# Gate rows by a DRAM round trip, shift and scale columns by sums with ones and a DRAM turn

## The chip, the cores and the metric

The kernel runs on one core of one Trainium2 chip. The metric is the device time of one execution in microseconds (us). The core has engines that run side by side, each in the order of its own list of instructions: TensorE (PE, matrix products, with its weight loads shown apart as PEld), VectorE (DVE), ScalarE (ACT), GpSimd (POOL) and SyncE (SP), which here does no arithmetic and issues nearly all DMAs. Tiles live in SBUF (128 partitions); products land in PSUM, which is read by DVE and ACT. DRAM is reached by DMA alone.

## The reference

The computation is a backbone of two layers over 1024 latent tokens and 256 context tokens, 1024 channels wide, in 32-bit floats. Layer 0 mixes tokens by windowed attention, layer 1 by gated linear attention; each is followed by a squared-ReLU MLP with 4096 hidden channels. What matters for the change is the modulation. Each layer has six vectors of 1024 numbers for each of two streams (latent and context tokens): shift, scale and gate for the mixer, and shift, scale and gate for the MLP.

```python
def modulate(x, gain, shift, scale):
    return rms_norm(x, gain) * (1 + scale) + shift

m_lat = jnp.split((c_lat @ w_mod[i] + b_mod[i])[:, None, :], N_MOD, axis=-1)   # c_lat = silu(c)
m_ctx = jnp.split(c_con @ w_mod[i] + b_mod[i], N_MOD, axis=-1)                 # c_con = silu(c_ctx)
h_lat = modulate(x_lat, g_pre_mix[i], m_lat[0], m_lat[1])
x_lat = x_lat + m_lat[2] * rms_norm(y_lat, g_post_mix[i])
f_lat = channel_mlp(modulate(x_lat, g_pre_mlp[i], m_lat[3], m_lat[4]), w_mlp_in[i], w_mlp_out[i])
x_lat = x_lat + m_lat[5] * rms_norm(f_lat, g_post_mlp[i])
```

Context tokens go through the same with `m_ctx` in layer 0; layer 1 needs of them only what its mixer reads. The output is the latent stream.

## The kernel before

**How the work is staged.** Tokens are handled in ten tiles of 128 (two of context, eight latent). The stages follow one another: the first modulation vectors and the query, key and value projections; attention over blocks of 128 queries; the output projection of attention; the first MLP, hidden part and then output part; layer 1's gates, projections, backward and forward scan; its output projection; the second MLP. Large products are made from operands that are split in a high and a low part (`split`, L211: ACT makes the high part, DVE the rest) and take three products each (`mm3`, L225: lines 228, 229 and 230). The MLPs use seven products of quarters in place of eight.

**The modulation vectors.** Only the first two (shift and scale of layer 0's mixer) are needed at once and are made by products with the weight (`mod_first`, L363); the change doesn't touch them. The other ten are made beside other work by `mod_sums` (L287): for vector j of layer l, eight slices of the weight, 128 rows by 1024 columns (512 KB), are loaded one after the other (L297), and DVE adds each, times the 128 numbers of the conditioning vector that belong to its rows, to an accumulator of 128 x 1024 for each stream (L308, L310). The vector itself is the sum of an accumulator over its 128 partitions. Vectors 0 to 2 of a layer belong to its mixer, 3 to 5 to its MLP, in the order shift, scale, gate. All vectors of layer 0 and vectors 0 and 1 of layer 1 have two streams, the others one. `mod_sums` is a generator: each `next` gives the place in the program of one step. Vectors 2, 3 and 4 of layer 0 are made during projections and attention, vector 5 and all six of layer 1 during the hidden part of the first MLP, with the last step in its output part.

**Shift and scale** (`mod_columns`, L320) are needed with channels on the partitions, as 8 columns of 128 for each stream. Eight blocks of an accumulator are transposed on PE against the identity into two PSUM banks (L331), DVE sums each bank along its free axis (L332), and then adds the bias (L336) and, for a scale, one and the gain (L339). They are read by `modulated` (L429), which normalises and transposes a tile and applies them.

**Gates** (`mod_gate`, L342) are needed as rows over channels, the same in all partitions. Four products with a 128 x 32 tile of ones (L355) put the two halves of each stream's sum into four groups of 32 partitions of one PSUM bank; a vector with one stream is put there twice. DVE adds the bias and multiplies by the post-norm gain (L359, L360), which have been loaded into the same places (L353, L354), and leaves the tile `gm`. When a gate is wanted, `gate_rows` (L406) spreads a row over 128 partitions: a product of one column of the identity, repeated 128 times, with `gm` copies one row of it into all rows of a PSUM bank (L414), and ACT copies that bank into the tile `row` (L415), twice for a row of 1024. It is called six times: for both streams at the end of attention (`o_ready`), for both in the first MLP's output part (`gla_first`), and for the latent stream in layer 1's last scan and in the second MLP's output part. The rows are read by DVE at L470 (`post_norm`), L1852, L2018 and L2027.

**What sets the order.** Outside two stretches the program's order is only a priority: a planner with a model of the engines' times works out, from data and buffers, which instruction each engine takes next, so that a later one can come ahead of an earlier one that isn't ready. Its places are fixed when the kernel is built. The first stretch (the first projections, up to about 65 us) is in written order on all engines, the second (the last projections) on PE alone. In the MLPs the priority itself comes from a list of due times (`Timeline`, L77): a step's operands are to be split 5.2 us before its products (L1085), its weights loaded 8 us before that. SP's list holds loads of weights and tiles, stores of hidden values, and the DMAs of the modulation alike. Buffers are shared: 45 slots of 128 x 1024 (`u`), six half tiles of 128 x 512 (`half`), and in PSUM four single banks (`ps1`) and two double ones (`ps2`). In the output parts of the MLPs `bank` takes half of a double one.

Of the kernel before, what the change touches and what calls it, by code (L numbers as in the profile page):

```python
# [11 lines left out]
F32 = mybir.dt.float32  # L12
F32R = mybir.dt.float32r
AF = mybir.ActivationFunctionType
ALU = mybir.AluOpType
# [3 lines left out]
P = 128  # L19
# [145 lines left out]
class Backbone:  # L165
# [121 lines left out]
    def mod_sums(self, vectors, apart=False):  # L287
# [29 lines left out]
                self.mod_gate(l, j // 3, acc) if j % 3 == 2 else self.mod_columns(l, j, acc)  # L317
        yield

    def mod_columns(self, l, j, acc):  # L320

        nc = self.nc
        which = j // 3
        out = self.const([P, 2, KT], f"{'SG'[j % 3]}{l}{which}")
        for s, a in enumerate(acc):
            col = out[:, s, :]
            for q in range(2):
                pt = self.bank("modT")
                for c in range(4):
                    kk = 4 * q + c  # L330
                    nc.tensor.transpose(pt[:, P * c : P * (c + 1)], a[:, P * kk : P * (kk + 1)], self.ident)  # L331
                nc.vector.tensor_reduce(  # L332
                    out=col[:, 4 * q : 4 * (q + 1)], in_=pt.rearrange("p (c k) -> p c k", c=4), op=ALU.add,
                    axis=mybir.AxisListType.X,
                )
            nc.vector.tensor_tensor(col, col, self.bcol[:, l, KT * j : KT * (j + 1)], op=ALU.add)  # L336
            if j % 3 == 1:
                c0 = 16 * which + 8 * l
                nc.vector.scalar_tensor_tensor(col, col, 1.0, self.cols[:, c0 : c0 + KT], ALU.add, ALU.mult)  # L339
        self.pre.setdefault((l, which), [None, None])[1 - j % 3] = out  # L340

    def mod_gate(self, l, which, acc):  # L342

        nc, t = self.nc, self.t
        bias, gain = self.half("brow"), self.half("gp")
        c0 = D * (3 * which + 2)
        key = ("g_post_mix", "g_post_mlp")[which]
        ps = self.bank("mod")
        for s in range(2):
            for h in range(2):  # L350
                r = 32 * (2 * s + h)
                cs = slice(512 * h, 512 * (h + 1))
                nc.sync.dma_start(bias[r : r + 32, :], t["b_mod"][l, c0 : c0 + D][cs].partition_broadcast(32))  # L353
                nc.sync.dma_start(gain[r : r + 32, :], t[key][l, cs].partition_broadcast(32))  # L354
                nc.tensor.matmul(  # L355
                    ps[r : r + 32, :], self.ones, acc[s % len(acc)][:, cs], start=True, stop=True, tile_position=(0, r)
                )
        gm = self.const([P, 512], f"gm{which}")
        nc.vector.tensor_tensor(gm, ps, bias, op=ALU.add)  # L359
        nc.vector.tensor_tensor(gm, gm, gain, op=ALU.mult)  # L360
        self.gm[l, which] = gm

    def mod_first(self):  # L363

# [40 lines left out]

    def gate_rows(self, l, which, s):  # L406

        nc = self.nc
        gm = self.gm[l, which]
        row = self.u(s="grow")  # L410
        for j in range(2):
            r = 32 * (2 * s + j)
            pb = self.bank("grow")
            nc.tensor.matmul(pb, self.ident[:, r : r + 1].to_broadcast([P, P]), gm, start=True, stop=True)  # L414
            nc.scalar.copy(row[:, 512 * j : 512 * (j + 1)], pb)  # L415
        return row


# [1676 lines left out]
```

## Time and profile before

| | |
|---|---|
| median of 3 runs | 2607.4 us (2607.23 to 2610.37) |
| profiled execution | 2610.2 us, its span from first to last instruction 2608.5 us |
| granted clock of PE | 0.994 |
| busy: PE, PEld, DVE, ACT, POOL | 97%, 81%, 66%, 48%, 17% of the span |
| DMA | 348.62 MB, mean 134 GB/s |
| products with the identity for gate rows (L414) | 24 records, median 592 ns |
| transposes of accumulators (L331) | 80 records, median 272 ns |
| products with ones (L355) | 32 records, median 605 ns |
| DVE sums of transposed accumulators (L332) | 20, median 0.67 to 0.69 us |
| ACT copies of gate rows (L415) | 12, median 588 ns |

A row of a group names the line, the engine, the operation, what is written and read, and how often; then come times in ns. In a row of the timeline the start and the length come first, in us. In a row of waits the engine that waited stands first and what released it behind the arrow, then the total in us, how often, and the longest. A product of 32-bit floats that are not split leaves two records. Matmuls overlap one another, so the sum of their lengths is more than the time that they take up.

### The profile page before, as it was taken

The numbers are of one execution on the slowest core, as the hardware profiler recorded it, in microseconds if no ns is written. First come the engines' busy times: TensorE is split into PE (matmuls) and PEld (weight loads), VectorE is DVE, ScalarE is ACT, GpSimd is POOL, SyncE is SP. The second block draws the span as 40 slices with busy tenths as digits, with TensorE's granted clock in tenths as the row PEclk, the third lists the DMA queues.
The fourth block names the chain that finished last, engine by engine and source line by source line (L and its number), as shares of the span: only waits on it lengthen the run. The fifth ranks groups of instructions, "written<-read, shape, count | busy, mean of one in ns | idle before, by whom it ended". The sixth has DMA issues, their size and how long they took to land.

```text
span 2608.5 us, 36262 instructions
## 1 busy us (share of the span) xinstructions
PE 2543.1 (97%) x13523; PEld 2116.2 (81%) x13523; DVE 1714.7 (66%) x2607; ACT 1258.2 (48%) x2356; POOL 430.8 (17%) x720
## 2 busy tenths in 40 slices
PE   7999999999999999999999999999998999999998
PEld 5778888888888888788878888888887888878886
DVE  4775888757767665758868625636658656566676
ACT  3345777744644444433325535334446545445333
POOL 0354666411000000000002212212310000000002
PEclk9999999999999999999999999999999999999999
DMA  9210011222455565837245331102321554567474
GB/s 312 89 65 33 26 56 54 82 81 85 145 158 158 183 209 167 292 113 266 89 147 193 129 91 51 32 18 97 97 97 49 180 160 134 177 246 235 161 226 161
DMA packets 229856, 348.62 MB, mean 134 GB/s; under 512 B 24600, under 2 KB 123184, under 8 KB 229680
## 3 DMA queue, kind: packets, MB, share of 16 engines
q1 hardware_dynamic: 227088, 336.87, 39.8%
q0 software_dynamic: 2592, 9.44, 0.9%
q8 instruction: 106, 1.74, 0.3%
q14 instruction: 70, 0.57, 0.1%
HBM read 270.75 MB, written 75.50 MB: 133 GB/s over the span
## 4 chain that ended last, share of the span: by engine, by line
PE 85%; DVE 5%; DMA 4%; ACT 2%; issue 2%; POOL 1%; SPq 1%; DVEq 0%; POOLq 0%; ACTq 0%
PE p L229 7%; PE p L228 7%; PE p L230 6%; PE pa L229 4%; PE pa L228 4%; PE pa L230 4%; PE o L802 3%; PE y L230 3%; PE y L228 3%; PE y L229 3%; PE rp L228 2%; PE rp L229 2%; PE rp L230 2%; PE pc L228 2%; PE pc L230 2%; PE pt L783 2%
## 5 line engine op out<-in xcount | busy, mean ns | idle before, releaser
L229 PE MATMUL p<-ol,oh 128*128 128x512 f32 x896 | 350.7, 391 | 0.1
L230 PE MATMUL p<-oh,ol 128*128 128x512 f32 x896 | 347.2, 391 | 0.0
L228 PE MATMUL p<-oh 128*128 128x512 f32 x896 | 329.6, 392 | 4.9 <-ACT oh L212 4.1
L241 POOL TENSOR_SCALAR rs<-ss 128x1 f32<-128x1 f32 (+1 forms) x78 | 26.5, 340 | 1641.9 <-ACT later L235 1458.9
L213 DVE TENSOR_TENSOR ol<-wh,oh 128x1024 fp32r<-128x1024 f32 x128 | 153.5, 1222 | 94.3 <-ACT oh L212 93.9
L228 PEld LDWEIGHTS p<-oh 128*128 128x128 f32 x896 | 168.6, 189 | 44.1 <-ACT oh L212 5.4
L229 PEld LDWEIGHTS p<-ol,oh 128*128 128x128 f32 x896 | 168.9, 189 | 36.5 <-DVE ol L213 1.0
L230 PEld LDWEIGHTS p<-oh,ol 128*128 128x128 f32 x896 | 168.9, 189 | 35.3 <-issue 0.2
L212 ACT CAST oh<-wh 128x1024 fp32r<-128x1024 f32 x128 | 131.4, 1050 | 132.0 <-DVE wh L1212 27.6
L310 DVE SCALAR_TENSOR_TENSOR ma<-wm,cT,ma 128x1024 f32<-128x1024 f32 x112 | 147.2, 1345 | 47.0 <-DMA wm<-in_w_mod 47.0
L212 ACT CAST oh<-k 128x1024 fp32r<-128x1024 f32 x96 | 98.0, 1053 | 127.3 <-DMA k<-in_w_mlp_out 60.2
L213 DVE TENSOR_TENSOR wi<-wi,wi 128x512 fp32r<-128x512 f32 x176 | 116.6, 688 | 47.3 <-ACT wi L212 45.5
L1042 ACT COPY s<-pa 128x512 f32<-128x512 f32 x96 | 56.0, 585 | 185.5 <-PE pa L230 185.4
L767 POOL TENSOR_SCALAR pr<-pr,den 128x640 f32<-128x640 f32 (+2 forms) x160 | 124.3, 790 | 29.4 <-DVE den L765 16.6
L213 DVE TENSOR_TENSOR ol<-k,oh 128x1024 fp32r<-128x1024 f32 x96 | 113.9, 1224 | 21.2 <-ACT oh L212 17.3
L212 ACT CAST wi<-wi 128x512 fp32r<-128x512 f32 x176 | 103.4, 615 | 34.7 <-DMA hd<-h 20.9
L755 ACT ACTIVATE pr<-pr,nm 128x640 f32<-128x640 f32 (+1 forms) x128 | 102.5, 802 | 28.2 <-DVE nm L750 26.3
L228 PE MATMUL y<-woh,oh 128*128 128x512 f32 x288 | 113.9, 396 | 0.0
L230 PE MATMUL y<-woh,ol 128*128 128x512 f32 x288 | 112.4, 391 | 0.9 <-DVE ol L213 0.9
L229 PE MATMUL y<-wol,oh 128*128 128x512 f32 x288 | 112.2, 390 | 0.0
L229 PE MATMUL rp<-wgl,ah 128*128 128x512 f32 x288 | 112.1, 390 | 0.0
L230 PE MATMUL rp<-wgh,al 128*128 128x512 f32 x288 | 111.9, 390 | 0.0
(391 smaller groups left out, 6745.3 us busy)
## 6 DMA issues: line engine op xcount, KB each, us to landing
wm<-in_w_mod SPq DMA_DIRECT2D x96, 512.0 KB, 4.4
hd<-h SPq DMA_DIRECT2D x80, 512.0 KB, 3.0
wh<-hd SPq DMA_DIRECT2D x144, 256.0 KB, 3.7
wh<-in_w_mlp_out SPq DMA_DIRECT2D x144, 256.0 KB, 4.2
wi<-in_w_mlp_in SPq DMA_DIRECT2D x64, 512.0 KB, 5.0
k<-hd SPq DMA_DIRECT2D x80, 256.0 KB, 5.4
k<-in_w_mlp_out SPq DMA_DIRECT2D x80, 256.0 KB, 5.4
x<-in_x SPq DMA_DIRECT2D x16, 512.0 KB, 4.3
```

What stands on the lines that cost most here:

```text
L212: self.nc.scalar.copy(hi, src)
L213: self.nc.vector.tensor_tensor(lo, src, hi.bitcast(F32), op=ALU.subtract)
L228: mm(out, a[0], b[0], start=start, stop=False, skip_group_check=onto)
L229: mm(out, a[0], b[1], start=False, stop=False, skip_group_check=onto)
L230: mm(out, a[1], b[0], start=False, stop=stop, skip_group_check=onto)
L241: nc.gpsimd.tensor_scalar(r, ss, inv_n, EPS, ALU.mult, ALU.add)
L310: nc.vector.scalar_tensor_tensor(acc[s], raw, c, acc[s], ALU.mult, ALU.add)
L755: nc.scalar.activation(pr, pr, AF.Exp, bias=nm[:, e : e + 1], scale=-1.0, accum_out=sums[:, e : e + 1])
L767: nc.gpsimd.tensor_scalar(pr, pr, den[:, e : e + 1], 0.0, ALU.mult, ALU.add)
L783: nc.tensor.transpose(pt[:, P * j : P * (j + 1)], probs[e][:, P * kt : P * (kt + 1)], self.ident)
L802: nc.tensor.matmul(po[64 * e : 64 * (e + 1), P * i4 : P * (i4 + 1)], self.kv[tile_i // 2][:, tile_i % 2, 256 + HD * g : 256 + HD * (g + 1) ...
L1042: nc.scalar.copy(s["s", j], s["pa"])
```

## The change

Shift and scale vectors are summed over the partitions by products with ones, as gates are (`mod_rows`). ACT copies the bank into a half tile, one row of each group of 32 is stored to a DRAM tile of 2 x 2 x 512 (`to_dram`, one DMA of 2 KB for each row), and one DMA for each stream loads it back with channels on the partitions. Bias, one and gain follow as before. The transposes and the sums on DVE are gone.

Gates are stored to DRAM the same way once bias and gain are in. `gate_rows` is one DMA that reads the 4 KB of a stream into all 128 partitions; the products with columns of the identity and the copies on ACT are gone. A gate with one stream now fills two groups of partitions and not four, and loads half the bias and gain rows. `gm` was a constant tile and is now one of the half tiles. All new DMAs are issued by SP.

```diff
+    def mod_rows(self, acc):
+
+        ps = self.bank("mod")
+        for s, a in enumerate(acc):
+            for h in range(2):
+                r = 32 * (2 * s + h)
+                self.nc.tensor.matmul(
+                    ps[r : r + 32, :], self.ones, a[:, 512 * h : 512 * (h + 1)], start=True, stop=True, tile_position=(0, r)
+                )
+        return ps
+
+    def to_dram(self, rows, n):
+
+        d = self.dp.tile([2, 2, 512], F32, name=self.nm("md"))
+        for r in range(2 * n):
+            self.nc.sync.dma_start(d[r // 2, r % 2 : r % 2 + 1, :], rows[32 * r : 32 * r + 1, :])
+        return d
+
     def mod_columns(self, l, j, acc):
 
         nc = self.nc
-        which = j // 3
+        which, n = j // 3, len(acc)
         out = self.const([P, 2, KT], f"{'SG'[j % 3]}{l}{which}")
-        for s, a in enumerate(acc):
+        rows = self.half("mrow")
+        nc.scalar.copy(rows[: 64 * n], self.mod_rows(acc)[: 64 * n])
+        d = self.to_dram(rows, n)
+        for s in range(n):
             col = out[:, s, :]
-            for q in range(2):
-                pt = self.bank("modT")
-                for c in range(4):
-                    kk = 4 * q + c
-                    nc.tensor.transpose(pt[:, P * c : P * (c + 1)], a[:, P * kk : P * (kk + 1)], self.ident)
-                nc.vector.tensor_reduce(
-                    out=col[:, 4 * q : 4 * (q + 1)], in_=pt.rearrange("p (c k) -> p c k", c=4), op=ALU.add,
-                    axis=mybir.AxisListType.X,
-                )
+            nc.sync.dma_start(col, d[s].rearrange("h (k p) -> p (h k)", p=P))
             nc.vector.tensor_tensor(col, col, self.bcol[:, l, KT * j : KT * (j + 1)], op=ALU.add)
...
     def mod_gate(self, l, which, acc):
 
         nc, t = self.nc, self.t
-        bias, gain = self.half("brow"), self.half("gp")
+        n = len(acc)
+        bias, gain, gm = self.half("brow"), self.half("gp"), self.half("gm")
         c0 = D * (3 * which + 2)
         key = ("g_post_mix", "g_post_mlp")[which]
-        ps = self.bank("mod")
-        for s in range(2):
+        for s in range(n):
             for h in range(2):
                 r = 32 * (2 * s + h)
                 cs = slice(512 * h, 512 * (h + 1))
                 nc.sync.dma_start(bias[r : r + 32, :], t["b_mod"][l, c0 : c0 + D][cs].partition_broadcast(32))
                 nc.sync.dma_start(gain[r : r + 32, :], t[key][l, cs].partition_broadcast(32))
-                nc.tensor.matmul(
-                    ps[r : r + 32, :], self.ones, acc[s % len(acc)][:, cs], start=True, stop=True, tile_position=(0, r)
-                )
-        gm = self.const([P, 512], f"gm{which}")
-        nc.vector.tensor_tensor(gm, ps, bias, op=ALU.add)
-        nc.vector.tensor_tensor(gm, gm, gain, op=ALU.mult)
-        self.gm[l, which] = gm
+        m = slice(0, 64 * n)
+        nc.vector.tensor_tensor(gm[m], self.mod_rows(acc)[m], bias[m], op=ALU.add)
+        nc.vector.tensor_tensor(gm[m], gm[m], gain[m], op=ALU.mult)
+        self.gm[l, which] = self.to_dram(gm, n)
...
     def gate_rows(self, l, which, s):
 
-        nc = self.nc
-        gm = self.gm[l, which]
         row = self.u(s="grow")
-        for j in range(2):
-            r = 32 * (2 * s + j)
-            pb = self.bank("grow")
-            nc.tensor.matmul(pb, self.ident[:, r : r + 1].to_broadcast([P, P]), gm, start=True, stop=True)
-            nc.scalar.copy(row[:, 512 * j : 512 * (j + 1)], pb)
+        self.nc.sync.dma_start(row, self.gm[l, which][s].rearrange("h c -> (h c)").partition_broadcast(P))
         return row
```

## The prediction

> **What bounds the kernel now.** I read the totals and the chain of waits first, then the busy times by stage, then the single instructions that the change touches, and last the waits of TensorE (PE), VectorE (DVE) and the DMA queue of SyncE (SP).
>
> ```profile
> span 2608.5 us, 36262 instructions
> ...
> PE 2543.1 (97%) x13523; PEld 2116.2 (81%) x13523; DVE 1714.7 (66%) x2607; ACT 1258.2 (48%) x2356; POOL 430.8 (17%) x720
> ...
> PE 85%; DVE 5%; DMA 4%; ACT 2%; issue 2%; POOL 1%; SPq 1%; DVEq 0%; POOLq 0%; ACTq 0%
> ...
> 0.00:65.00 65.00, 49.48 (x417) 37.18 (x418) 30.89 (x71) 24.47 (x40) 4.44 (x22) 0.97 1.01 313
> ...
> 355.00:505.00 150.00, 146.91 (x1395) 125.41 (x1392) 123.59 (x262) 114.32 (x292) 90.41 (x165) 1.00 0.21 58
> ...
> 600.00:1050.00 450.00, 443.84 (x2343) 378.38 (x2342) 305.59 (x414) 226.53 (x420) 7.51 (x17) 1.00 0.51 160
> ...
> 1050.00:1380.00 330.00, 325.22 (x1420) 264.60 (x1419) 235.67 (x280) 124.28 (x133) 0.00 (x0) 1.00 0.53 182
> ...
> 2560.00:2608.00 48.00, 38.80 (x170) 31.46 (x168) 32.18 (x39) 14.12 (x26) 9.32 (x16) 0.96 0.57 203
> ```
>
> The last five rows are stages: their length, then busy time of PE, weight loads, DVE, ACT and POOL. PE is idle for 2608.5 - 2543.1 = 65.4 us, and the first and last stage hold 15.5 and 9.2 of them, which the change doesn't touch. In the 2495 us between it is idle for 40.7 us, 1.6%. So what PE no longer has to do should come off the end nearly one for one, as long as nothing else becomes late; DVE, 82% busy in the attention stage (355 to 505) and 68% in the first MLP, is the next.
>
> **What is removed from PE.** Busy time can't be added up here, since matmuls overlap; I take the distance from start to start, set against the 0.23 us at which the split weight products follow one another.
>
> ```profile
> L414 PE MATMUL grow<-gm,ident x24: 591/592/696, 501.4 to 2278.8; 128*128 128x512 f32 x24
> 501.36 3.70 PE L414 MATMUL grow<-gm,ident 128*128 128x512 f32 x8
> 504.89 0.82 PE L783 MATMUL pt<-ident,pr 128*128 128x128 f32 x6
> L331 PE MATMUL modT<-ident,ma x80: 270/272/329, 365.8 to 990.1; 128*128 128x128 f32 x80
> 953.40 0.39 PE L230 MATMUL pa<-o4h,wi 128*128 128x512 f32 x1
> 953.63 1.03 PE L331 MATMUL modT<-ident,ma 128*128 128x128 f32 x8
> ...
> 954.73 0.39 PE L229 MATMUL pa<-o6l,wi 128*128 128x512 f32 x1
> ```
>
> The 12 products with a column of the identity are 24 records. Eight of them hold PE from 501.36 to 504.89, 3.53 us, or 0.43 to 0.44 each: 24 x 0.43 = **-10.3 us**. Eight transposes push the second product behind them from 953.40 + 2 x 0.23 = 953.86 to 954.73: 0.87 us, 0.109 each, so 80 x 0.109 = **-8.7 us**.
>
> **What is added to PE.** The sum over partitions with ones is an operation the gates already do.
>
> ```profile
> 1359.26 0.39 PE L230 MATMUL p<-oh,ol 128*128 128x512 f32 x1
> 1359.58 1.05 PE L355 MATMUL mod<-ma,ones 128*32 128x512 f32 x4
> 1360.56 0.50 PE L228 MATMUL p<-oh 128*128 128x512 f32 x1
> 1360.89 0.39 PE L229 MATMUL p<-ol,oh 128*128 128x512 f32 x1
> 911.41 1.07 PE L355 MATMUL mod<-ma,ones 128*32 128x512 f32 x8
> 912.40 0.50 PE L228 MATMUL pc<-o3h,wi 128*128 128x512 f32 x1
> 912.74 0.39 PE L229 MATMUL pc<-o3l,wi 128*128 128x512 f32 x1
> ```
>
> Two products (four records) and four products (eight records) both hold PE for 0.98 to 0.99 us: products into different groups of 32 output rows run side by side. With the slower product behind it a piece costs 1360.89 - (1359.26 + 2 x 0.23) = 1.17, say 1.2 us. Six vectors get one (shift and scale of the MLP of layer 0, and of both halves of layer 1). If the four products of a vector with two streams stay together this is 6 x 1.2 = 7.2 us; if all four such vectors fall apart into pairs, 4 x 2.4 + 2 x 1.2 = 12.0. The gate at 911 stayed together, the one at 1359 came apart. I take together for the four vectors in the MLP stage, where 911 lies, and pairs for the two in attention, without the slower neighbour: 4 x 1.2 + 2 x 2.0 = **+8.8 us**. The last gate (layer 1, one stream) now has two products where it came in two pieces: **-1.2 us**. The other gate of layer 1 drops from four to two in one piece: nothing. Sum on PE: -10.3 - 8.7 - 1.2 + 8.8 = **-11.4**.
>
> [...]
>
> **Waits that go.**
>
> ```profile
> PE px L228 <- ACT grow L415: 1.5, 1, 1.5
> PE pt L783 <- DVE S L332: 0.7, 1, 0.7
> L332 DVE TENSOR_REDUCE S<-modT x10: 671/684/686, 369.2 to 955.4; 128x4 f32<-128x512 f32 x10
> L415 ACT COPY grow<-grow x12: 572/588/604, 502.5 to 2500.9; 128x512 f32<-128x512 f32 x12
> ```
>
> Both name removed instructions: **-2.2 us**. DVE loses 20 reductions of 0.68 us (13.7 us), ACT loses 12 copies and gains 6 of the same size. I count these at nothing: they lie beside PE's 98% in their stages. At the rate at which PE feels DVE's waits in the first MLP (13%, below) they would be worth 1.8 us more.
>
> **The DMAs that come.** 20 row stores of 2 KB, 10 column loads (1024 single floats each), 12 gate-row stores, 6 broadcasts of 512 KB, minus 8 bias and gain loads: 40 more issues on SP, which also issues every weight load.
>
> ```profile
> hc<-hx SPq DMA_DIRECT2D x64, 64.0 KB, 1.8
> gd<-in_gla_w_gate_down SPq DMA_DIRECT2D x8, 64.0 KB, 3.8
> x<-in_x SPq DMA_DIRECT2D x16, 512.0 KB, 4.3
> L339 DVE SCALAR_TENSOR_TENSOR G<-G,cols x5: 166/167/206, 501.2 to 993.6; 128x8 f32<-128x8 f32 x5
> L470 DVE TENSOR_TENSOR xo<-y,grow x18: 1214/1224/1226, 525.2 to 1968.6; 128x1024 f32<-128x1024 f32 x18
> 540.33 0.90 ACT L457 ACTIVATE h<-xt,S,G 128x128 f32<-128x128 f32 x2 [4.71 <-PE xt L438]
> SPq L1073 <- ACT hx L1004: 82.9, 25, 10.6
> DVE ma L310 <- DMA wm<-in_w_mod: 46.5, 29, 3.3
> ```
>
> A broadcast costs about what loading x does, 4.3 us, and its first use lies 525.2 - 502.5 = 22.7 us after the copy it replaces: hidden, also if it takes five times that. A store to DRAM lands after 1.8 us (64 KB row); the nearest row for a column load is the gate-down weight, 1024 pieces of 64 bytes, 3.8 us; a single float may go faster or, unseen, far slower. So columns come some 1.8 + 3.8 plus 1.6 to 2 of issue, 7 to 8 us, after the ACT copy. The MLP's scale columns are finished from 501.2 on now, and their first reader, at 540.3, is 39 us later.
>
> What can hurt is the queue. SP waits for ACT's copy, then for the store's landing, and behind it stand the next slice of the modulation weight (L297), MLP weights (L979) and hidden stores. DVE's addition of the bias waits for the column, and behind it stand the accumulations (L310) and splits (L213) that PE needs. The planner places an instruction where it expects it to be ready, so only its error counts. SP already waits for ACT 82.9 us in 25 places of the first MLP (the row before last), and DVE for a slice 46.5 us in 29, at most 3.3 each; PE loses 450.0 - 443.8 = 6.2 us there, 13% of what DVE waits. Six vectors at 3.3 us each give 19.8 on DVE and, at 13%, **+2.6 us**; the bounds are nothing and the second rival's 24.
>
> **Sum:** -11.4 - 2.2 + 2.6 = -11.0. The profiled execution took 2610.2 us (1.7 around its span), so 2599.2 for it; the median shown is 2.8 lower, so **2596.4** for the median, -0.4%. By stage: attention -3.7, first MLP's hidden part -0.4 (transposes -5.2, sums +4.8), its output part -6.1, the two places of layer 1 -1.7 each, and the 2.6 in the first two.
>
> **The rivals.**
>
> *The new order eats the gain.* From 65 us on the planner works out every place anew, and a freed PE slot is worth something only if the next operands are there.
>
> ```profile
> PE p L228 <- ACT oh L212: 4.1, 2, 2.6
> PE pa L228 <- ACT wi L212: 3.6, 2, 1.8
> PE pa L228 <- ACT o6h L212: 3.0, 1, 3.0
> 1243.32 1.02 PE L414 MATMUL grow<-gm,ident 128*128 128x512 f32 x2
> ```
>
> Waits of PE are few and single, up to 3 us; three or four more such would take the 11 us: 2607, no change. For it: six of the products, as at 1243, were placed long before their use, as fillers where the planner saw a hole. Against it: on the chip PE had no hole there. Chance 0.13.
>
> *DVE held by the columns (slower).* If the additions are placed as though a column were there at once, DVE stands for the whole 8 us, six times. The cover is the planned lead of the MLP's splits, 5.2 us ahead of their products (L1085).
>
> ```profile
> L213 DVE TENSOR_TENSOR wi<-wi,wi 128x512 fp32r<-128x512 f32 x176 | 116.6, 688 | 47.3 <-ACT wi L212 45.5
> L212 ACT CAST wi<-wi 128x512 fp32r<-128x512 f32 x176 | 103.4, 615 | 34.7 <-DMA hd<-h 20.9
> ```
>
> A split takes 0.6 + 0.7 = 1.3 us of it, so 3.9 us are covered and PE loses 4: 6 x 4 = 24, against -13.6 without the other waits: 2607.4 - 13.6 + 24 = 2618. It decides from a hold of 3.9 + 13.6/6 = 6.2 us per vector. For it: DVE is in order. Against it: no wait of DVE for a slice is above 3.3 us. Chance 0.08.
>
> *The columns themselves are slow.* [...] Chance 0.04. [...]
>
> **Range and chances.** Forecast 0.75, rivals 0.13, 0.08 and 0.04. A measurement of this kernel tells about 0.2% (5.2 us) from no change, so faster means below 2602.2: 0.75; same 0.13; slower 0.12. Low end: all sums together (7.2, not 8.8: -1.6), no added wait (-2.6), 1.8 more from DVE, and an order that is luckier by some 4: 2586. High end: all in pairs (+3.2) and the better half of the first rival: 2608. The forecast's own range is 2586 to 2602.
>
> **What would show it.** Right: no transposes of the accumulators and no products with the identity for rows, 64 records of products with ones instead of 32, PE busy time lower and its idle time between 65 us and the last stage near 40; DVE waits for column loads of 20 us or less in all; broadcasts land in 4 to 5 us. Wrong: column loads landing after tens of us, DVE waits of over 5 us per vector for them, weight slices waited for longer than 46.5 us in the first MLP, or the first MLP's hidden part longer by more than 3 us.

## The result and the profile after

The changed kernel takes 2595.1 us (median of 5 runs, 2591.74 to 2597.13) against 2607.4 for the kernel before (5 runs beside them, 2605.4 to 2610.37): ratio 0.995, 95% interval 0.9939 to 0.9961. The forecast was 2596.4. Of the six executions of rows_only below, one took 2821.9 us against 2592.2 to 2598.2 for the others, and it is left out of that version's median and ratio.

The first listing has the totals of the changed kernel and the stretch of its span from 65 us to the last stage: length, then busy time of PE, weight loads, DVE, ACT and POOL.

```profile
span 2595.4 us, 36179 instructions
...
PE 2529.4 (97%) x13451; PEld 2105.8 (81%) x13451; DVE 1703.1 (66%) x2587; ACT 1255.6 (48%) x2350; POOL 435.2 (17%) x720
...
65.00:2545.00 2480.00, 2437.87 (x12851) 2034.08 (x12850) 1638.96 (x2477) 1215.64 (x2282) 420.24 (x682) 0.99 0.40 129
```

The span is 13.1 us shorter. PE is busy 13.7 us less, and its idle time is 66.0 us, as good as the 65.4 of before; in the stretch shown it is 2480.0 - 2437.9 = 42.1, against 40.7 before. So in total PE's work came off the end one for one. The stages will show that this total hides larger terms of both signs.

The next two listings are from the groups by tile: the bank `mod` with its copy `mrow`, and the DRAM tiles `md` with those who waited for them.

```profile
L326 PE MATMUL mod<-ma,ones x64: 592/605/617, 127.0 to 1346.0; 128*32 128x512 f32 x64
...
L344 ACT COPY mrow<-mod x6: 568/582/592, 367.6 to 979.9; 128x512 f32<-128x512 f32 x4, 64x512 f32<-64x512 f32 x2
```

```profile
L335 SPq DMA_DIRECT2D md<-mrow x20: 233/245/253, 368.3 to 980.8; - x20
...
L419 SPq DMA_DIRECT2D grow<-md x6: 319/351/529, 497.1 to 2485.6; - x6
...
  DVE G L349: 3.1, 4
  DVE S L349: 1.5, 2
```

There are 64 records of products with ones, the transposes of accumulators and the products with the identity for rows are gone, and DVE waited 4.6 us in six waits for columns in the whole run. How long a broadcast takes to land, for which the prediction had 4 to 5 us, the profile doesn't record.

One column path in the timeline of the changed kernel, with the products that it stands between:

```profile
803.55 0.28 PE L230 MATMUL px<-ah,wi 128*128 128x256 f32 x1
...
803.76 1.06 PE L326 MATMUL mod<-ma,ones 128*32 128x512 f32 x8
...
804.75 0.50 PE L228 MATMUL pc<-o3h,wi 128*128 128x512 f32 x1
...
804.91 0.59 ACT L344 COPY mrow<-mod 128x512 f32<-128x512 f32 x1 [0.97 <-PE mod L326]
805.09 0.39 PE L229 MATMUL pc<-o3l,wi 128*128 128x512 f32 x1
...
805.53 1.12 SPq L335 DMA_DIRECT2D md<-mrow  x4
...
807.00 0.39 SPq L348 DMA_DIRECT2D S<-md  x1
...
809.20 0.17 DVE L349 TENSOR_TENSOR S<-S,bcol 128x8 f32<-128x8 f32 x1 [0.68 <-DMA S<-md]
```

Four products with ones are eight records in one piece, and the next product starts 0.99 us after them. The stores go out at 805.53, the load (of one stream's 1024 single floats) at 807.00, and DVE, which waited for it, starts at 809.20: 3.7 us from the first store and 2.2 from the load's issue.

For the stages I took the start of the first product of each (the first into `y`, then into `pa`, into the MLP's `p`, and so on; the last stage ends with the start of PE's last product) in two profiles of each kernel, the second being the runs before_again and after_again below. Lengths in us:

```
                    before   again | after    again | change of mean | forecast
up to output proj.   506.9   505.8 | 499.9    497.2 |     -7.8       |  -3.7
output projection    123.6   123.6 | 125.9    125.6 |     +2.2       |   0
first MLP, hidden    416.3   415.0 | 410.7    409.1 |     -5.8       |  -0.4
first MLP, output    400.9   402.6 | 396.7    397.6 |     -4.6       |  -6.1
layer 1 mixer        420.4   420.3 | 420.5    420.5 |     +0.2       |  -1.7
its output proj.     101.1   101.1 | 102.7    102.7 |     +1.6       |   0
second MLP, hidden   319.3   317.4 | 315.6    315.5 |     -2.8       |  -1.7
second MLP, output   310.6   309.5 | 314.2    314.6 |     +4.4       |   0
```

The +2.6 us of added waits stood beside the first and the third row. Two profiles of one kernel differ by up to 2.7 us in the first stage and by up to 1.9 in the others, so a change of under 2 us is taken as real only where the two profiles agree. Part of that difference may be the clock: without the last 20 us, the granted clock of PE is 0.50 in seven stretches of the first profile of before and in eight of the first of after, each 3.41 us long but for one of 6.83 in either profile. In the stretch from 1855.51 of after weight products follow one another at 0.43 us, and at 0.23 behind it. Layer 1's output projection takes 102.5 to 102.8 us with such a stretch and 101.1 or 101.2 without, so I put one at some 1.3 to 1.7 us; the section on the hardware has the rows.

### The profile page after: what moved, and what is told of

It reads as the page before. It is cut to its first block, busy times and chain, and to the rows that moved or that the text cites. A ratio compares the mean times of both kernels' runs of the same rounds, so it can differ in the third digit from the quotient of the medians.

```text
span 2595.4 us, 36179 instructions
## 1 busy us (share of the span) xinstructions
PE 2529.4 (97%) x13451; PEld 2105.8 (81%) x13451; DVE 1703.1 (66%) x2587; ACT 1255.6 (48%) x2350; POOL 435.2 (17%) x720
## 5 line engine op out<-in xcount | busy, mean ns | idle before, releaser
L229 PE MATMUL p<-ol,oh 128*128 128x512 f32 x896 | 349.8, 390 | 0.2
L228 PE MATMUL p<-oh 128*128 128x512 f32 x896 | 329.3, 392 | 8.6 <-ACT oh L212 5.4
L228 PEld LDWEIGHTS p<-oh 128*128 128x128 f32 x896 | 168.3, 188 | 47.0 <-ACT oh L212 8.6
L212 ACT CAST oh<-wh 128x1024 fp32r<-128x1024 f32 x128 | 131.5, 1050 | 154.5 <-DVE wh L1216 34.9
L229 PEld LDWEIGHTS p<-ol,oh 128*128 128x128 f32 x896 | 168.6, 188 | 36.4 <-DVE ol L213 1.5
L228 PE MATMUL y<-woh,oh 128*128 128x512 f32 x288 | 115.0, 400 | 2.5 <-ACT woh L212 1.3
L759 ACT ACTIVATE pr<-pr,nm 128x640 f32<-128x640 f32 (+1 forms) x128 | 102.5, 802 | 28.3 <-DVE nm L754 26.9
L229 PE MATMUL y<-wol,oh 128*128 128x512 f32 x288 | 112.6, 392 | 0.1
L229 PE MATMUL rp<-wgl,ah 128*128 128x512 f32 x288 | 112.0, 390 | 0.0
```

Of the source, the lines that this page charges most:

```text
L212: self.nc.scalar.copy(hi, src)
L228: mm(out, a[0], b[0], start=start, stop=False, skip_group_check=onto)
L229: mm(out, a[0], b[1], start=False, stop=False, skip_group_check=onto)
L759: nc.scalar.activation(pr, pr, AF.Exp, bias=nm[:, e : e + 1], scale=-1.0, accum_out=sums[:, e : e + 1])
```

## The experiments

All times are medians beside runs of the kernel before on the same chip (2606.4, 2607.9 and 2607.8 in the three groups).

| run | us | ratio to before, 95% |
|---|---|---|
| rows_only | 2595.6 | 0.9957 (0.9945 to 0.9970) |
| cols_only | 2600.6 | 0.9973 (0.9963 to 0.9983) |
| reductions_kept | 2598.8 | 0.9972 (0.9963 to 0.9980) |
| second_hop | 2595.2 | 0.9957 (0.9945 to 0.9969) |
| after_again | 2593.7 | 0.9951 (0.9937 to 0.9964) |
| rows_late | 2592.1 | 0.9943 (0.9930 to 0.9955) |
| rows_late_again | 2593.0 | 0.9942 (0.9928 to 0.9956) |
| pe_turn | 2595.5 | 0.9947 (0.9935 to 0.9960) |
| late_pe_turn | 2595.7 | 0.9954 (0.9941 to 0.9966) |
| one_store | 2595.6 | 0.9955 (0.9942 to 0.9967) |
| before_again | 2606.6 | one execution |

**rows_only: the gates alone.** The columns are made as before.

```diff
-        rows = self.half("mrow")                      # changed mod_columns
-        nc.scalar.copy(rows[: 64 * n], self.mod_rows(acc)[: 64 * n])
-        d = self.to_dram(rows, n)
...
+        nc.tensor.transpose(pt[:, P * c : P * (c + 1)], a[:, P * kk : P * (kk + 1)], self.ident)
+        nc.vector.tensor_reduce(out=col[:, 4 * q : 4 * (q + 1)], in_=pt.rearrange("p (c k) -> p c k", c=4), ...)
```

> The gate half of the change alone: gates go through DRAM and are spread by one DMA; shift and scale columns are made as before, with 80 transposes and 20 DVE reductions. Theory (PE's own time is what counts): products with the identity -10.1 us measured from start to start, last gate in one piece -1.2, wait for the copy of a gate row -1.5: -12.8, some 2594.6 us, ratio 0.995. Rival (much of the gain came from the columns, by DVE's relief or by the planner's new order, since the first MLP's hidden part alone got 5.7 us shorter): -6 to -8, some 2600, ratio 0.997 to 0.998. PE idle time stays near 65 us by the theory.

Measured: 2595.6, 10.8 us below the kernel before beside it (2606.4). The interval of the ratio is 7.8 to 14.3 us and holds the 12.8 of PE's account. The first MLP's hidden part keeps its length (414.1 against 416.3 and 415.0), its output part is 392.5, the shortest of all.

**cols_only: the columns alone.** `mod_gate` and `gate_rows` are those of before; the excerpt shows the second of them against the changed kernel.

```diff
-        self.nc.sync.dma_start(row, self.gm[l, which][s].rearrange("h c -> (h c)").partition_broadcast(P))
+        for j in range(2):
+            r = 32 * (2 * s + j)
+            pb = self.bank("grow")
+            nc.tensor.matmul(pb, self.ident[:, r : r + 1].to_broadcast([P, P]), gm, start=True, stop=True)
+            nc.scalar.copy(row[:, 512 * j : 512 * (j + 1)], pb)
```

> The column half alone: shift and scale by sums with ones and a DRAM turn; gates stay in a constant tile and are spread by 12 products with the identity and 12 ACT copies as before. Theory (PE's own time): transposes -8.7, six sums +7.0, wait for a reduction -0.7: -2.4, some 2605 us, ratio 0.999, not to be told from no change. Rival (DVE's relief or order): the hidden part of the first MLP is shorter by 5 to 6 us as in the whole change, and the time by 5 to 6: 2602, ratio 0.998.

Measured: 2600.6, 0.9973 (4.4 to 9.6 us faster). The 2.4 that PE's account gave lie outside that; the rival's 5 to 6 lie inside. Much of the gain is in the hidden part: 409.8 us against 415 to 416. The profiled execution, at 2596.7 us the fastest of its seven, has the stage up to the output projection 5 us shorter as well (501.3), so this one profile shows more than the median gains. And the halves don't add up: by the ratios 11.2 and 7.0 are 18.2 us, where both together gave 13.0 and 12.8 (after, after_again). The intervals all but allow that, but two places show that something is given back only with both. The output projection takes 123.1 us with the gates alone, 123.6 with the columns alone, 125.9 and 125.6 with both; rows_late below goes into it. The first MLP's output part takes 392.5 with the gates alone and 400.1 with the columns alone against a mean of 401.8 before, so 9.3 and 1.7 less, but 396.7 and 397.6 with both, 4.6 less; why is open.

The waits of PE from 600 to 1050 us, first in the kernel before, then in its second profile, then in the changed kernel, show where a good part of the hidden part's gain came from:

```profile
PE pc L228 <- DVE s L1046: 2.0, 1, 2.0
PE pa L228 <- ACT wi L212: 1.8, 1, 1.8
PE pc L228 <- ACT wi L212: 0.7, 1, 0.7
PE pc L230 <- DVE wi L213: 0.6, 1, 0.6
```

```profile
PE pc L228 <- DVE s L1046: 2.0, 2, 1.8
...
PE pc L228 <- ACT wi L212: 0.8, 1, 0.8
PE pc L230 <- DVE wi L213: 0.8, 1, 0.8
```

```profile
PE pa L228 <- ACT wi L212: 1.8, 1, 1.8
PE pa L229 <- DVE o6l L213: 0.5, 1, 0.5
PE px L228 <- ACT hx L1038: 0.5, 1, 0.5
```

Three kinds of wait, 3.3 us in one profile of before and 3.6 in the other, are not there in the changed kernel; the other 2 us or so of the gain they don't explain. The largest follows a slice of the modulation weight that landed late: DVE stood in its accumulation, the sum `s` was behind it on DVE, and PE needed `s`.

**reductions_kept: is it that DVE has less to do?** The 20 reductions of before run again, on the bank `mod`, with their result unused.

```diff
+        ps = self.mod_rows(acc)
+        idle = self.small(4, "idle")
+        for _ in range(2 * n):
+            nc.vector.tensor_reduce(out=idle[: 64 * n], in_=ps[: 64 * n].rearrange("p (c k) -> p c k", c=4),
+                                    op=ALU.add, axis=mybir.AxisListType.X)
```

> The changed kernel with DVE's 20 reductions of a 128 x 512 PSUM bank put back (13.7 us of DVE work whose result nobody reads, so the output is the same). Theory (DVE's work lies beside PE): 2595 us, within 2 us of the changed kernel, first MLP's hidden part within 1 us of 410.7. Rival (DVE's relief took the 3.4 us of idle PE time from the hidden part): hidden part about 414 us, time 2597 to 2599, and DVE's waits or PE's waits for DVE and ACT grow by that.

Measured: 2598.8, ratio 0.9972, some 4 to 5 us above the changed kernel; but not in the way that either account had it. The hidden part is 409.7, as short as without the reductions. In the profiled execution, the slowest of the ten at 2603.4 us, the clearest loss lies at the output projection: it takes 129.1 us (125.9 and 125.6 without). The waits of ACT and PE for its weights, and the stretch behind them with its granted clock:

```profile
ACT woh L212 <- DMA wor<-in_attn_w_o: 13.0, 3, 11.7
...
PE y L228 <- ACT woh L212: 3.2, 1, 3.2
```

```profile
511.50:518.50 7.00, 5.42 (x26) 4.09 (x26) 4.65 (x5) 5.05 (x6) 0.00 (x0) 0.53 0.52 161
```

PE waits 3.2 us for the first weights, where the changed kernel waits 1.3 (below), and over the 7.0 us shown the granted clock is 0.53, where the same stretch of the changed kernel has 1.00. So in this execution a longer wait at one place, and the lower clock behind it, are the largest part of the loss; how much of that stands behind the median isn't shown, nor why the wait is longer. That DVE's relief shortens the hidden part is out.

**second_hop: what the column path costs.** One more DMA, from DRAM to DRAM, lengthens every column's way.

```diff
-        d = self.to_dram(rows, n)
+        first = self.to_dram(rows, n)
+        d = self.dp.tile([2, 2, 512], F32, name=self.nm("md2"))
+        nc.sync.dma_start(d[:n], first[:n])
```

> The changed kernel with one more DMA between the store and the load of the columns (DRAM to DRAM, 4 or 8 KB), so that a column comes some 2 us later and SP waits once more for each vector. Theory (the path of the columns is hidden and the planner counts with it): within 2 us of 2595. Rival (a hold of DVE passes on at 13%, or SP's wait delays the weight slices): 6 x 2 us x 13% = +1.6 at least, up to 6 x 2 = +12 if all of it reaches PE: 2597 to 2607, and DVE's waits for columns grow from 4.6 us.

Measured: 2595.2, ratio 0.9957 against 0.9950 and 0.9951 for the changed kernel: no difference that can be told, but the rival's lowest figure, 1.6 us, can't be told from nothing either. DVE's waits for the columns in that kernel, then a wait of PE in the first MLP's hidden part:

```profile
DVE G L351 <- DMA G<-md: 9.3, 4, 5.9
...
DVE S L351 <- DMA S<-md: 5.0, 5, 2.0
```

```profile
PE mod L326 <- DVE ma L310: 1.4, 1, 1.4
```

The waits for columns rise from 4.6 to 14.3 us, one of them to 5.9. The hidden part takes 412.1 us, the longest of the ten profiles with summed columns and 2.2 above the mean of after and after_again; PE has 2.3 us of waits there that the changed kernel doesn't have, the one shown and 0.9 us for the sum `s`. In the total this doesn't show: the output projection (124.3) and that of layer 1 (101.2, at full clock) are shorter than in the changed kernel. So the way of a column through DRAM costs little, but one profile says that it is not quite free in the MLP, and that a longer one is felt there.

**rows_late: what is given back at the output projection.** In the changed kernel the two broadcasts for the attention's gate stand on SP's queue ahead of the output projection's weights. First SP's issues in the changed kernel, then the waits for those weights there:

```profile
497.09 0.51 SPq L419 DMA_DIRECT2D grow<-md  x1
497.71 0.37 SPq L348 DMA_DIRECT2D G<-md  x1
498.17 0.53 SPq L419 DMA_DIRECT2D grow<-md  x1
498.75 1.48 SPq L482 DMA_DIRECT2D x<-in_ctx  x1
500.28 3.80 SPq L220 DMA_DIRECT2D wor<-in_attn_w_o  x6
```

```profile
ACT woh L212 <- DMA wor<-in_attn_w_o: 11.1, 3, 9.9
...
PE y L228 <- ACT woh L212: 1.3, 1, 1.3
```

The broadcasts themselves are wanted only at 520.5. The experiment calls them after the loop over the query blocks, so that the weights come first.

```diff
-            ready["rows"] = [self.gate_rows(0, 0, s) for s in range(2)]
...
-        rows = ready["rows"]
+        rows = [self.gate_rows(0, 0, s) for s in range(2)]
```

> The changed kernel with the two gate-row broadcasts of layer 0's mixer asked for after the attention loop instead of in its last round, so that on SP's list they stand behind the loads of the output projection's weight and not ahead of them. Theory (in the changed kernel the 1 MB of broadcasts goes ahead of the weight; ACT waits 11.1 us for it and PE 1.3 for ACT): PE's wait for the split weight goes, the stretch from the first output product to the first MLP product is 2 us shorter, time 2593, 1 to 2 us below the changed kernel. Rival (that wait is hidden or moves on): same as the changed kernel, 2595. A new risk: rows come too late for the first residual at about 520, then DVE waits for them and it gets slower.

SP's issues, and ACT's wait, in that kernel:

```profile
496.48 4.46 SPq L220 DMA_DIRECT2D wor<-in_attn_w_o  x6
501.04 1.76 SPq L419 DMA_DIRECT2D grow<-md  x2
```

```profile
ACT woh L212 <- DMA wor<-in_attn_w_o: 7.6, 3, 6.4
```

The six loads are issued 3.8 us earlier (1.9 of it because the stage before ended earlier), ACT's wait falls by 3.5, PE's wait for `woh` is gone, and the output projection takes 123.7 us instead of 125.9 and 125.6. The total is 2592.1.

The broadcasts alone don't cost this. In rows_only they stand ahead of the weights too:

```profile
493.55 0.84 SPq L424 DMA_DIRECT2D grow<-md  x2
...
497.66 4.11 SPq L220 DMA_DIRECT2D wor<-in_attn_w_o  x6
```

There the weights go out 5.8 us before the stage's first product, and the stage takes 123.1 us; in pe_turn, also without columns through DRAM, it is 123.1 as well. In cols_only, with columns and without broadcasts, they go out 4.6 us before it. In the changed kernel the broadcasts and the loads of the columns alternate, and the weights go out 0.4 us after the stage's first product. So the loss seems to take both halves of the change, which fits that it shows only with both.

**rows_late_again**, the same kernel on another chip, to see whether that holds.

> The kernel with the late broadcasts once more, on the chip of the next one. Theory (the collision with the output weight cost 2 us): 2592 to 2593 again, no wait of PE for the split output weight. Rival: its first 2592.1 was luck, 2594 to 2595.

It took 2593.0, with the stage at 123.7 again. The ten executions of both have a mean of 2592.8, the ten of after and after_again of 2594.4. The intervals of the ratios overlap, so the 1.6 us rest on the stage, which both pairs of profiles show (-2.1), more than on the totals. Its medians are the lowest here.

**after_again** repeats the changed kernel in the group of rows_late, pe_turn and one_store.

> The changed kernel once more, on the chip of the other three, as their measure, and for how much the stages of one kernel differ from one profiled execution to the next. All theories: 2595 us, ratio 0.995 to 0.996; each stage within 1 us of the first profile of it, if the differences between kernels are to be read from one profile each.

It took 2593.7; its stages stand in the table above. Two of them differ from those of the first profile by more than the 1 us expected: the first by 2.7 and the first MLP's hidden part by 1.6.

**pe_turn: the rows turned on PE.** The columns are summed with ones, copied by ACT, and then turned by four products with the identity instead of DRAM.

```diff
-        d = self.to_dram(rows, n)
...
-            nc.sync.dma_start(col, d[s].rearrange("h (k p) -> p (h k)", p=P))
+        pt = self.bank("modT")
+        for k in range(4):
+            nc.tensor.transpose(pt[:, P * k : P * k + 64 * n], rows[: 64 * n, P * k : P * (k + 1)],
+                                self.ident[: 64 * n, : 64 * n])
```

> The changed kernel with the DRAM turn of shift and scale replaced: the summed rows, copied to SBUF as there, are transposed on PE in four blocks a vector (both streams at once) and DVE adds the bias straight from PSUM; gates as in the change. Theory (PE's own time): 24 transposes at 0.109 = +2.6, with the edges of six groups up to +3.5: 2598, about 3 above the changed kernel. Rival 1 (the DRAM round trip itself costs, through SP's list or DVE's waits of 4.6 us): no slower than the changed kernel, 2594 to 2595. Rival 2 (the columns gained more than PE's time because accumulators and banks are held for a shorter time): the hidden part of the first MLP stays as short as in the change, within 2 us, plus 4 x 0.5.

Measured: 2595.5, 1.8 above after_again beside it, with intervals that overlap. This alone would settle nothing, but the hidden part is 411.3, near the changed kernel and not near the 415 to 416 of before, though no column goes through DRAM here. So the short hidden part isn't owed to the DRAM trip.

**late_pe_turn**: the same edit on top of rows_late, beside rows_late_again.

> Late broadcasts and the turn on PE together. Theory (PE's own time, +2.6 to +3.5 for 24 transposes): 2595, some 3 above the kernel with the late broadcasts. Rival (the DRAM round trip costs as much as the transposes): 2592, within 1 us of it.

Measured: 2595.7 against 2593.0 for rows_late_again, 2.7 us longer. That fits the 2.6 us of 24 added transposes on PE, but the intervals of the ratios overlap.

**one_store: one DMA for all rows of a vector** (10 stores in place of 32).

```diff
-        for r in range(2 * n):
-            self.nc.sync.dma_start(d[r // 2, r % 2 : r % 2 + 1, :], rows[32 * r : 32 * r + 1, :])
+        self.nc.sync.dma_start(d[:n].rearrange("s h c -> (s h) c"), rows[0 : 64 * n : 32, :])
```

> The changed kernel with one DMA for the two or four rows of a vector in place of two or four (22 issues on SP fewer, about 0.28 us each). Theory (SP's time is not on the path): same as the changed kernel, 2595, within 2 us. Rival (SP's issue time holds the weight slices behind it): 2593 or less, and DVE's waits for slices lower than the 40.6 us of the changed kernel.

Measured: 2595.6 against 2593.7 for after_again beside it, no difference that can be told and none in the rival's direction. Nothing here says that the number of issues on SP costs time.

**before_again: does the wait in the hidden part belong to before, or to one execution?**

> The kernel before once more, for a second profile of it. In its first profile PE waits 2.0 us near 939 for a DVE sum that stands behind a late slice of the modulation weight, and PE's clock is halved from 942 to 945.5. Theory (that wait belongs to the order of the kernel before): the second profile shows a wait of PE of 1 to 2 us at the same sum, and its first MLP's hidden part is 414 to 417 us long against 409 to 411 in the kernels with the new columns. Rival (chance of one execution): no such wait, hidden part 412 or less, and the gain there in the changed kernel was no gain of the change.

The wait at `s` came again (2.0 us in two, shown above) and the hidden part took 415.0, so it belongs to the order of the kernel before. What didn't come again is what followed it. First two stretches of 3.41 us of the kernel before (the wait, and behind it), then two of its second profile; behind the five busy times stands the granted clock:

```profile
938.78:942.19 3.41, 1.40 (x7) 1.16 (x7) 1.98 (x3) 1.37 (x3) 0.00 (x0) 1.00 0.72 221
942.19:945.60 3.41, 3.41 (x10) 2.64 (x9) 2.97 (x4) 1.62 (x4) 0.00 (x0) 0.50 0.79 244
```

```profile
935.72:939.13 3.41, 2.07 (x18) 1.87 (x16) 2.12 (x3) 0.00 (x0) 0.00 (x0) 1.00 0.59 186
939.13:942.54 3.41, 2.99 (x13) 2.49 (x14) 1.54 (x3) 2.94 (x6) 0.00 (x0) 1.00 0.91 263
```

The same wait was followed by 3.41 us at a granted clock of 0.50 in one execution, and by 1.00 in the other (1.00 throughout from 934 to 947 us). The stretches are cut as in the last section: in the first execution the wait lies in one of them, in which PE is busy for 1.40 us, and in the second it falls across two, with 2.07 and 2.99.

## Why the prediction was right, and where it was not

**The work taken from PE: right.** Measured on their places in the kernel before, the transposes took 8.7 us and the products for rows 10.1, and the last gate saved its second piece. The rows' gain shows in rows_only, and the first MLP's output part is 396.3 us in the mean of the ten profiles without these products against 401.2 in the three with them: 4.9, where the forecast had 6.1.

**The sums with ones: mis-sized.** Of the step "four together, two in pairs, 8.8" the pairs were wrong: all six vectors came in one piece. The size of one, from the timeline above: without the sum, L228 would start 0.12 behind the narrow product at 803.55 and L229 0.23 later, at 803.90; it starts at 805.09, 1.19 later. Such a piece is 1.2 us in the MLP and about 1.05 in attention, 6.9 for six, near the low bound of the step (7.2) and not the value taken.

With that, PE's account is -10.1 - 8.7 - 1.2 + 6.9 = -13.1, and its busy time fell by 13.7.

**Waits: the sum was right, the places were not.** The forecast was -2.2 for two waits that go and +2.6 for added ones, +0.4 together, and PE's idle time rose by 0.6. But it is made of other things than the steps said:

- *First MLP's hidden part.* Forecast -0.4 and a part of the +2.6; measured -5.8. The step that failed is "six vectors at 3.3 us each ... at 13%": in the changed kernel no wait was added, though second_hop shows that longer columns do bring some back. DVE's wait for slices of the modulation weight fell from 46.5 to 38.5 us, in this row of the changed kernel,

```profile
DVE ma L310 <- DMA wm<-in_w_mod: 38.5, 27, 3.3
```

and three kinds of wait of PE went, 3.3 to 3.6 us of the 5.8. All ten profiles with summed columns have this part at 409.1 to 412.1, the three without at 414.1 to 416.3. It isn't DVE's relief (reductions_kept, 409.7) and not the trip through DRAM (pe_turn, 411.3). What is left is the order that the planner works out when ten pairs of banks of transposes are replaced by one bank of sums per vector, or the accumulators' earlier release; these two I have not told apart.

- *Output projection.* "A broadcast ... hidden, also if it takes five times that" looked only at who waits for the broadcast. What mattered is who stands behind it: the six weight loads on the same queue, which the columns' DMAs had already made late. With the broadcasts behind them the stage is 2.1 us shorter (rows_late). The prediction named SP's queue as what can hurt, but for the columns and not for the rows.

- *Layer 1.* Forecast -1.7 at the mixer, measured +0.2, and then +1.6 in the output projection behind it, which the forecast had at nothing. The products for that gate's rows lay in a hole of PE before. Waits of PE from 1800 to 1900 us in the changed kernel:

```profile
PE y L228 <- DVE on L1663: 1.2, 1, 1.2
...
PE oo L1642 <- DVE on L1663: 0.7, 1, 0.7
```

Neither row is among the waits of the kernel before in that stretch: the 1.7 us of products became waits of 1.9. The first rival said that some products were fillers, and the prediction answered that PE had no hole there; at this place it had one. And behind the hole, now empty, the granted clock is 0.50 in six of the ten profiles without these products (after, after_again, reductions_kept, one_store, rows_late, rows_late_again), and 1.00 in second_hop, pe_turn and late_pe_turn; in the six the output projection takes 102.5 to 102.8 us, in the four others 101.1 or 101.2, as in the three with the products. That is the +1.6, which so belongs to the executions that were profiled as much as to the kernel.

- *Second MLP's output part.* Forecast 0, measured +4.4. With the hidden part in front of it the whole MLP changes by +1.6, where the two profiles of before differ by 3.0, so part of this may be a shift between the two parts. PE's waits from 2180 to 2560 us and ACT's for the weights, first before, then changed:

```profile
PE p L228 <- ACT oh L212: 2.6, 1, 2.6
...
ACT oh L212 <- DMA k<-in_w_mlp_out: 38.5, 13, 5.7
```

```profile
PE p L228 <- ACT oh L212: 3.9, 3, 2.5
...
ACT oh L212 <- DMA k<-in_w_mlp_out: 42.9, 13, 5.7
```

PE waits 1.3 us more for split weights and ACT 4.4 us more for the DMAs that bring them: freed time that turns into waits for operands, the first rival's mechanism once more. No run tests it by itself, and PE's waits shown account for only 1.3 of the 4.4; the rest is open.

- *Up to the output projection.* Forecast -3.7, measured -7.8. Some 1.9 of it are the two sums in one piece. The rest is open; reductions_kept, 500.8 there against a mean of 498.6, could speak for DVE's relief, but two profiles of one kernel differ by as much, and pe_turn has 501.0 without the reductions.

**The rivals that fell.** DVE is hardly held by the columns: 4.6 us in all, and with 14.3 PE's waits grew by some 2 us in one stage (second_hop), not by the 24 of that rival. No run shows the slow columns to which the forecast gave 0.04: it is 3.7 us from the first store to the use and 4.3 from the start of the ACT copy, where the step had 7 to 8 from the copy, and the load of 1024 single floats in the timeline above took 2.2 us from issue to use.

So the sum over PE was nearly right (-11.4, measured -13.1), and it is about as large as the whole gain; but the closeness of the total, 2595.1 against 2596.4, is luck as well: of the rest, an unforeseen gain of some 9 us (first stage and hidden part) met losses of some 8 that the forecast had at nothing (both output projections and the last stage) and 1.9 at the layer 1 mixer. Nor did each half of the change give what PE's account has for it: the columns alone gave 7.0 by the ratio, where the account has 2.4. The first rival, at 0.13, has its mechanism at work in that mixer and, as far as the waits tell, in the last stage, and it took no more than a part of the gain.

## What to carry to other kernels

When PE is 97% busy, count the work that it loses from start to start, place by place; that gave the total here, though not the stages. Then ask of every added DMA not only when its own data is wanted but what stands behind it on its queue: a load that isn't urgent, issued ahead of one that other DMAs had already made late, cost 2.1 us and was mended by moving one call. And a product that was taken away at a place where the next operands weren't there yet left a wait of its own size here (1.9 us for 1.7), and in six of ten profiles a granted clock of 0.50 behind it, where the stage took 1.3 to 1.7 us more.

## What the runs showed of the hardware

The granted clock of PE, as the first profiles of the two kernels record it, is 0.50 in the stretches of this table (starts in us, the last 20 us left out). All are 3.41 us long, but those at 1993.49 and 1978.38 are 6.83:

| | starts | distances, in units of 3.413 us |
|---|---|---|
| before | 61.55, 140.06, 942.19, 1423.47, 1969.60, 1993.49, 2307.52 | 23, 235, 141, 160, 7, 92 |
| after | 60.09, 138.60, 254.66, 626.71, 1312.79, 1855.51, 1978.38, 2289.00 | 23, 34, 109, 201, 159, 36, 91 |

In these two profiles the distances are whole multiples to within 0.01 us. I cut both profiles at these multiples, without the first 12 and the last 20 us, and counted the stretches of 3.41 us at full clock by the share in which PE is busy:

| PE busy | stretches before, after | followed by a clock of 0.50 before, after |
|---|---|---|
| under 45% | 5, 6 | 5, 6 |
| 45 to 55% | 7, 5 | 2, 2 |
| over 55% | 734, 730 | 0, 0 |

In the middle row one and the same gap went both ways: 1.79 us of idle PE, all in one stretch (busy for 47.5%), was followed by 1.00 in before (gap at 628.65) and by 0.50 in after (gap at 624.02). What decides there isn't shown.

The hole at 1853 us in the changed kernel and the stretch behind it, then the same place in the program (some 15 us later) in the kernel before, where the products for rows start at 1854.65 and 1858.10:

```profile
1852.09:1855.51 3.42, 1.27 (x6) 0.46 (x5) 3.42 (x7) 2.83 (x8) 1.92 (x2) 1.00 0.45 153
1855.51:1858.92 3.41, 3.41 (x9) 2.65 (x10) 3.41 (x7) 0.00 (x0) 0.38 (x1) 0.50 0.00 0
```

```profile
1867.20:1870.62 3.42, 2.53 (x13) 1.84 (x13) 3.42 (x7) 2.74 (x7) 1.25 (x2) 1.00 0.49 153
1870.62:1874.03 3.41, 3.41 (x16) 2.82 (x16) 3.41 (x7) 0.01 (x1) 0.00 (x0) 1.00 0.03 5
```

PE is busy for 1.27 of 3.42 us in the first and for 2.53 in the other. In second_hop the hole is as large as in the changed kernel (PE busy for 1.85 of the 4.00 us from 1850.60, and for 1.84 of the 4.00 us from 1851.70 in the changed kernel), and the clock behind it is 1.00. So the size of a gap alone didn't tell whether the clock was lower behind it. That it matters how much of one of these stretches a gap empties, and that this is luck where it could as well lie across two, is my reading of the counts and of the two profiles at 939 us; no run moves a gap to see.

Leaving out the last 20 us, where PE runs dry, the clock was at 0.50 for 27 us in the first profile of the kernel before and for 31 in that of the changed one; the places differ between executions of one kernel (942 us in before, none from 934 to 947 in before_again). Of nine executions of the kernel before on one chip (beside rows_late) the fastest took 2604.75 us at a mean granted clock of 0.996 and the slowest 2610.2 at 0.993; that the clock is the cause of the 4 to 5 us by which executions of one kernel differ here is argued, not shown. The gap of 1.57 us from 252.09 in the changed kernel, alone in its stretch, had a clock of 0.50 behind it.

The column of 1024 single floats that the timeline shows was in use 2.2 us after its load's issue (changed kernel, 807.00 to 809.20). In the changed kernel four products with ones into different groups of 32 rows held PE for 0.99 to 1.00 us in the four vectors with two streams, two for 0.98 us in the two with one.
